# Second half's loads and squares moved into the first half's block loop, six conditioning columns moved into the mixer, last three squares summed apart

## The chip, the core and the metric

The kernel runs on one core of a Trainium2 chip. The metric is the device time of one execution in microseconds (us). A core has a matrix engine (PE, with its weight loads listed as PEld), a vector engine (DVE), a scalar engine (ACT), a general engine (POOL) and SyncE (SP), which issues most DMA transfers here; POOL issues some too.

## What is computed

The reference is a trunk of two layers over one sequence of 1024 positions and 1024 features, in float32. A conditioning vector c gives every layer six vectors of 1024 (shift, scale and gate for the token mixer and for the MLP).

```
cond = silu(c)
mod  = cond @ w_mod[i] + b_mod[i]            # six vectors: sh_m, sc_m, gt_m, sh_f, sc_f, gt_f
h = rms_norm(x, g) * (1 + sc_m) + sh_m
y = mixer(h)                                  # layer 0: recurrent, layer 1: pooling
x = x + gt_m * y
h = rms_norm(x, g) * (1 + sc_f) + sh_f
x = x + gt_f * (relu(h @ w1)**2 @ w2)
...
return rms_norm(x, final_norm_g)

# recurrent mixer of layer 0
gate = gelu(h @ w_y + b_y);  xr = conv4(h @ w_in + b_in)
r, i = sigmoid(blockdiag(xr, w_a)), sigmoid(blockdiag(xr, w_x))
a = exp(8 * r * log_sigmoid(lam));  u = sqrt(1 - a*a) * i * xr
y = (scan(a, u) * gate) @ w_out + b_out
```

## The kernel before

x lies transposed: 128 partitions hold a block of features, and there are 8 blocks (k or m = 0 to 7). The 1024 positions are two halves of 512 (h = 0, 1; tiles xa and xb). Every product is made of three matmuls of 128x128 weights with 512 positions: high part by high part, high by low, low by high (mm3, L188 to L190; the input norm's own in L401). Weights come as raw tiles of 512 KB (pool rawp, three buffers, shared with the conditioning columns), ACT casts the high part and DVE subtracts the low part (split_part, L180 and L181).

**Start.** The first loop of loads (L113 to L129) issues on SP, in the order of a string, the w_in pieces for features k (w_k) and for each block e the two raw conditioning tiles mw[e] of 2 x 512 KB (scale, then shift). SP works its queue in order. The *block loop* (L380 to L402) then runs over the 8 blocks of half 0: DVE makes scale and shift of a block from mw[k] (scale_of and bias_of, L335 to L339), ACT makes hh (high part of the normalised block), DVE hl (low part), and PE adds the block's 18 matmuls into the six accumulators ps6. The helper `after` (L321 to L328) ties each instruction of ACT, DVE and POOL in this stretch to the one before it on its engine, so the order there is that of the code, and all these lines show as L328. POOL issues accumulating DMAs (tile k of w_k) meanwhile. Behind the block loop stand the loads and splits of w_in 6 and 7, load_x(1) (four loads of 512 KB for xb, L409), the squares of xb (s1, L443 to L445: ACT squares, DVE adds them up), the evictions of ps6 to xr (conv_input, L426), the products of w_in 6 and 7 for half 0 (proj), rstd_bcast of s1 (L265 to L289; 4 matmuls with a column of ones, square root, reciprocal, and two matmuls with a diagonal dg that spread it), norm_split (L291) and the products of half 1.

**Mixer.** The loop at L556 runs over four heads hd, and over both halves in each: gates (L502 to L540) makes four sigmoid gates from w_g, then a chain through ACT, POOL, DVE to the scan; gelu_block (L542 to L546) multiplies two blocks of w_y products, taken through gelu on ACT. A stage is written (hd, h). Each split_unit loads one weight tile and then calls drip(n) with n = rate[0]: n *conditioning columns* for later (mod_steps, L216; mod_column, L205 to L207) each take a raw buffer, one load of 512 KB (mb) on SP, and one DVE pass over 128x1024. Columns come in the order gate of the mixer (0,2), then (0,4), (0,3), (0,5) for the MLP, then layer 1. rate[0] is hd. Three units load per head, so 0, 3, 6 and 9 columns are made. Outside the tied stretch a scheduler orders the instructions of each engine by the code's order, by buffers and by data.

**MLP of layer 0.** The wo loop (L586 to L599) adds the mixer's product to x and sums squares (ss); f1(0, 0) at L858 makes the first hidden chunk, with ffn_norm of half 1 (L571) inside it, on ss[1]; its four weight loads drip one column each (f1_jobs, L682), and drip_until(0, 5) at L859 makes those that are missing of the MLP's gate.

**End.** The last product of half 1, last 256 positions, goes through last_chunk (L1013): xb is updated on DVE, squared on ACT, summed on DVE for the letters V of the plan; the last square (X) has a tile of its own. rstd_row (L993 to L1002) multiplies both tiles by a 128x128 of ones, and ACT and DVE make root and reciprocal over 128x256; final_norm scales and stores.

## Time and profile before

| what | value |
|---|---|
| times of 3 runs | 1739.61, 1742.8, 1742.51 us (median 1742.51) |
| the profiled execution's own time | 1740.37 us |
| its span in the trace | 1738.5 us |
| mean granted TensorE clock | 0.994 of full speed |
| PE busy | 1690.5 us, 97% |
| DVE, ACT, POOL busy | 1358.9, 967.2, 492.3 us |
| HBM read, written | 181.79 MB, 4.19 MB |

The trace is that of one execution. A row of a timeline has start, duration, engine, line, operation, output<-inputs, shapes and, in square brackets, the idle time of the engine ahead of it with what ended it. The span covers the first to the last instruction; the execution's own time is 1.87 us longer. PE is busy for 97% of the span, so what is idle of PE is some 48 us, in stretches that can be listed one by one.

### The profile page before, as it was taken

The numbers are of one execution on the slowest core, as the hardware profiler recorded it, in microseconds if no ns is written. First come the engines' busy times: TensorE is split into PE (matmuls) and PEld (weight loads), VectorE is DVE, ScalarE is ACT, GpSimd is POOL, SyncE is SP. The second block draws the span as 40 slices with busy tenths as digits, with TensorE's granted clock in tenths as the row PEclk, the third lists the DMA queues.
The fourth block names the chain that finished last, engine by engine and source line by source line (L and its number), as shares of the span: only waits on it lengthen the run. The fifth ranks groups of instructions, "written<-read, shape, count | busy, mean of one in ns | idle before, by whom it ended". The sixth has DMA issues, their size and how long they took to land.

```text
span 1738.5 us, 20871 instructions
## 1 busy us (share of the span) xinstructions
PE 1690.5 (97%) x7472; PEld 1386.7 (80%) x7472; DVE 1358.9 (78%) x2115; ACT 967.2 (56%) x1660; POOL 492.3 (28%) x419
## 2 busy tenths in 40 slices
PE   6899999999999999999999999999999999999997
PEld 4687778877788888888888888888878787878787
DVE  7897867589898989897973898559696868687847
ACT  6588886555454454545457787745444454545432
POOL 2132343103241414151416333303140405041403
PEclk9999999999999999999999999999999999999999
DMA  9423425642423333332319888841111112120202
GB/s 337 168 93 104 143 85 162 143 119 83 136 72 123 95 99 109 96 117 89 123 37 198 202 192 179 190 118 61 49 59 39 61 38 70 39 69 29 80 6 97
DMA packets 63175, 187.33 MB, mean 108 GB/s; under 512 B 6752, under 2 KB 9184, under 8 KB 63072
## 3 DMA queue, kind: packets, MB, share of 16 engines
q1 hardware_dynamic: 47376, 157.43, 27.6%
q0 software_dynamic: 15696, 28.58, 9.9%
q8 instruction: 58, 0.95, 0.2%
q14 instruction: 45, 0.37, 0.1%
HBM read 181.79 MB, written 4.19 MB: 107 GB/s over the span
## 4 chain that ended last, share of the span: by engine, by line
PE 75%; DVE 10%; issue 3%; ACT 3%; DMA 2%; POOL 1%; DVEq 0%; ACTq 0%; POOLq 0%
PE mm L188 25%; PE mm L189 25%; PE mm L190 25%; DMA mb<-in_wmod 2%; DVE mb L207 1%; DVE xa L773 1%; DVE xb L773 1%; POOL xa L782 1%; DVE xcb L440 1%; DVE w_a_s L181 1%; ACT c L777 0%; DVE gate L530 0%; PE sm L272 0%; DVE w_y L181 0%; DVE w_s L181 0%
## 5 line engine op out<-in xcount | busy, mean ns | idle before, releaser
L188 PE MATMUL mm<-hh,w_w 128*128 128x512 f32 x1024 | 399.7, 390 | 0.9 <-DVE xa L773 0.9
L189 PE MATMUL mm<-hl,w_w 128*128 128x512 f32 x1024 | 399.3, 390 | 0.0
L190 PE MATMUL mm<-hh,w_w 128*128 128x512 f32 x1024 | 399.0, 390 | 0.0
L782 POOL TENSOR_TENSOR xb<-xb,c 128x512 f32<-128x512 f32 x104 | 150.0, 1442 | 625.4 <-ACT c L777 625.2
L188 PEld LDWEIGHTS mm<-hh,w_w 128*128 128x128 f32 x1024 | 192.6, 188 | 43.1 <-DVE xa L773 3.0
L190 PEld LDWEIGHTS mm<-hh,w_w 128*128 128x128 f32 x1024 | 192.6, 188 | 40.2
L189 PEld LDWEIGHTS mm<-hl,w_w 128*128 128x128 f32 x1024 | 192.5, 188 | 39.5
L782 POOL TENSOR_TENSOR xa<-xa,c 128x512 f32<-128x512 f32 x104 | 159.7, 1535 | 145.2 <-ACT c L777 145.2
L777 ACT ACTIVATE c<-c,mod 128x512 f32<-128x512 f32 x104 | 75.3, 724 | 202.6 <-DVE c L803 135.5
L623 ACT ACTIVATE relu<-mm 128x512 f32<-128x512 f32 x128 | 76.2, 596 | 144.7 <-PE mm L190 144.7
L207 DVE SCALAR_TENSOR_TENSOR mb<-mb,cond 128x1024 f32<-128x1024 f32 x80 | 114.5, 1434 | 47.9 <-DMA mb<-in_wmod 47.9
L773 DVE SCALAR_TENSOR_TENSOR xa<-mm,mod,xa 128x512 f32<-128x512 f32 x156 | 113.0, 742 | 25.8 <-POOL xa L782 25.8
L181 DVE TENSOR_TENSOR w_w<-raw_w,w_w 128x512 fp32r<-128x512 f32 x112 | 106.8, 962 | 12.4 <-ACT w_w L180 12.4
L165 POOL DMA_DIRECT2D w_w<-in_w x80 | 70.5, 900 | 151.0 <-ACT w_w L164 120.6
L613 DVE TENSOR_TENSOR u<-usq,u 128x512 fp32r<-128x512 f32 x102 | 70.2, 688 | 16.1 <-ACT u L612 15.8
L188 PE MATMUL mm<-u,w_a_a 128*128 128x512 f32 x200 | 79.1, 396 | 2.3 <-DVE xb L773 1.2
L188 PE MATMUL mm<-u,w_w 128*128 128x512 f32 (+1 forms) x224 | 80.9, 361 | 0.0
L189 PE MATMUL mm<-u,w_w 128*128 128x512 f32 (+1 forms) x224 | 80.5, 360 | 0.1
L190 PE MATMUL mm<-u,w_w 128*128 128x512 f32 (+1 forms) x224 | 80.4, 359 | 0.0
L180 ACT CAST w_w<-raw_w 128x512 fp32r<-128x512 f32 x112 | 65.1, 612 | 25.0 <-PE mm L190 17.3
L189 PE MATMUL mm<-u,w_a_a 128*128 128x512 f32 x200 | 78.0, 390 | 0.0
L190 PE MATMUL mm<-u,w_a_a 128*128 128x512 f32 x200 | 77.9, 389 | 0.0
(326 smaller groups left out, 4030.0 us busy)
## 6 DMA issues: line engine op xcount, KB each, us to landing
raw_w<-in_w SPq DMA_DIRECT2D x148, 512.0 KB, 3.5
mb<-in_wmod SPq DMA_DIRECT2D x80, 512.0 KB, 3.8
w_w<-in_w POOLq DMA_DIRECT2D x80, 256.0 KB, 5.5
mw<-in_wmod SPq DMA_DIRECT2D x16, 512.0 KB, 11.0
raw_in<-in_w_in SPq DMA_DIRECT2D x8, 512.0 KB, 7.0
raw_y<-in_w_y SPq DMA_DIRECT2D x8, 512.0 KB, 3.7
raw_o<-in_w_out SPq DMA_DIRECT2D x8, 512.0 KB, 4.2
outT<-o SPq DMA_DIRECT2D x12, 256.0 KB, 2.2
```

The source lines that it names most:

```text
L165: nc.gpsimd.dma_start(w[:, 1, 0:n], src, accum_op=ALU.add)
L180: S.copy(w[:, 0, 0:n], raw)
L181: (eng or V).tensor_sub(w[:, 1, 0:n], raw, w[:, 0, 0:n].bitcast(F32))
L188: PE.matmul(out=ps, lhsT=wh, rhs=rh, start=first, stop=False)
L189: PE.matmul(out=ps, lhsT=wh, rhs=rl, start=False, stop=False)
L190: PE.matmul(out=ps, lhsT=w[:, 1, c:c + P], rhs=rh, start=False, stop=last)
L207: V.scalar_tensor_tensor(raw, raw, 1.0, cond, op0=ALU.mult, op1=ALU.mult, accum_out=m[:, e:e + 1])
L613: eng.tensor_sub(u[n][:, 1, jj, :], src, u[n][:, 0, jj, :].bitcast(F32))
L623: S.activation(r, ps, AF.Relu)
L773: V.scalar_tensor_tensor(xb, ps, g[:, r + 4 * row:r + 4 * row + 1], xb, op0=ALU.mult, op1=ALU.add)
L777: S.activation(t, src, AF.Identity, scale=g[:, r + 4 * row:r + 4 * row + 1])
L782: G.tensor_add(xb, xb, t)
```

## The change

Four edits. The four loads of xb are issued between mw5 and mw6 instead of behind the block loop. The squares of xb and their sums are made by square1 inside the block loop, at k = 5 (blocks 0 to 2), k = 6 (3 to 5) and k = 7 (6 and 7), tied by `after` to the loop's order. The mixer's rate per unit becomes 0, 2, 3, 3 (6 columns more in all), and the four units of f1(0, 0) drip none. In the last chunk the plan has three squares of their own (X); the new class LastSumSq multiplies the running sum and each of the three by a column of ones as they come, into one accumulator, and rstd_bcast (128x2 and the dg matmuls) takes the place of rstd_row.

```diff
--- before.py
+++ after.py
@@ -110,7 +110,7 @@
         return part * n, part * n + n
 
     mw = [slot(f"mw{e}", (2, D)) for e in range(NB)]
-    for what in "0ww1w2w34567":
+    for what in "0ww1w2w345x67":
         if what == "w":
             q = len(k_raw)
             if q == 0:
@@ -122,6 +122,8 @@
                 for r, c0 in ((r1, 0), (r2, D)):
                     lo, hi = piece(r, q, part)
                     nc.sync.dma_start(r[:, lo:hi], w_k[q, :, c0 + lo:c0 + hi])
+        elif what == "x":
+            load_x(1)
         else:
             e = int(what)
             for j in (1, 0):
@@ -248,6 +250,7 @@
             self.name, self.n, self.plan, self.room = name, n, plan, room
             self.parts = {}
             self.i = 0
+            self.ps = None
 
         def add(self, xb):
             who = self.plan[self.i]
@@ -262,15 +265,36 @@
                 S.activation(sq, xb, AF.Square)
                 return (G if who == "G" else V).tensor_add(a, a, sq)
 
+    class LastSumSq(SumSq):
+
+
+        def add(self, xb):
+            if self.i == 0:
+                self.ps = small_ps()
+            if self.plan[self.i] == "V":
+                super().add(xb)
+                if "V" in self.plan[self.i:]:
+                    return
+                a = self.parts["V"]
+            else:
+                a = tmp("sq", self.n)
+                self.i += 1
+                S.activation(a, xb, AF.Square)
+            for q in range(self.n // P):
+                PE.matmul(out=self.ps[:, q:q + 1], lhsT=a[:, q * P:(q + 1) * P], rhs=ones[:, 0:1],
+                          start=(a is self.parts["V"] and q == 0), stop=(self.i == NB), skip_group_check=True)
+
     def rstd_bcast(ss, trace=None):
 
         nq = ss.n // P
         parts = list(ss.parts.values())
-        ps = small_ps()
-        for q in range(nq):
-            for pi, a in enumerate(parts):
-                PE.matmul(out=ps[:, q:q + 1], lhsT=a[:, q * P:(q + 1) * P], rhs=ones[:, 0:1],
-                          start=(pi == 0), stop=(pi == len(parts) - 1))
+        ps = ss.ps
+        if ps is None:
+            ps = small_ps()
+            for q in range(nq):
+                for pi, a in enumerate(parts):
+                    PE.matmul(out=ps[:, q:q + 1], lhsT=a[:, q * P:(q + 1) * P], rhs=ones[:, 0:1],
+                              start=(pi == 0), stop=(pi == len(parts) - 1))
         r = mp.tile([P, 4], F32, tag="rstd", name="rstd", bufs=2)
         root = S.activation(r[:, 0:nq], ps[:, 0:nq], AF.Sqrt, bias=eps, scale=1.0 / D)
         V.reciprocal(r[:, 0:nq], r[:, 0:nq])
@@ -370,6 +394,15 @@
     def normed(k):
         xn[k] = tmp("xn")
         after(V.tensor_mul, xn[k], x[0][:, k, :], bc0)
+
+    s1 = SumSq("m01")
+
+    def square1(k):
+        sq = tmp("sq")
+        after(S.activation, sq, x[1][:, k, :], AF.Square)
+        a = s1.parts.setdefault("V", sq)
+        if a is not sq:
+            after(V.tensor_add, a, a, sq)
 
     low = prepare(0)
     bias_of(0)
@@ -395,6 +428,8 @@
             prepare(k + 1)
         if k + 3 < NB:
             normed(k + 3)
+        for k1 in {5: (0, 1, 2), 6: (3, 4, 5), 7: (6, 7)}.get(k, ()):
+            square1(k1)
         for low, r in ((0, hh), (0, hl), (1, hh)):
             for u in range(6):
                 w, c = (w1_, u * P) if u < 4 else (w2_, odd * 256 + (u - 4) * P)
@@ -406,7 +441,6 @@
         behind.enter_context(tc.issue_after(tail_of[e].ins))
 
     uin = {m: split_unit(w_in[m], f"in{m}") for m in (6, 7)}
-    load_x(1)
     xc = [Blocks("xca"), Blocks("xcb")]
     edge = const.tile([P, NB, 3], F32, name="edge")
     xr3 = []
@@ -440,9 +474,6 @@
                 V.scalar_tensor_tensor(o, xr[:, k:k + H], vcol(f"cw{k}", m), o,
                                        op0=ALU.mult, op1=ALU.add)
 
-    s1 = SumSq("m01", plan="VVVVVVVV")
-    for k in range(NB):
-        s1.add(x[1][:, k, :])
     xr = [conv_input(m, ps6[m], 0) for m in range(6)]
     taken = last_traced(S)
     xr.append(conv_input(6, proj(uin[6], hh[0], hl[0]), 0))
@@ -554,7 +585,7 @@
             V.tensor_sub(yl[h][:, k, :], xc[h][:, k, :], yh[h][:, k, :].bitcast(F32))
 
     for hd in range(4):
-        rate[0] = hd
+        rate[0] = (0, 2, 3, 3)[hd]
         ug = split_unit(w_g[hd], f"g{hd}")
         uy = [split_unit(w_y[m], f"y{m}") for m in (2 * hd, 2 * hd + 1)]
         for h in range(2):
@@ -680,7 +711,7 @@
     DRIPS = (1, 1, 1, 1, 1, 1, 1, 1)
 
     def f1_jobs(i, c, eng=None):
-        return [partial(lambda j: split_unit(w1[i, c * 4 + j], f"w1_{i}_{c}_{j}", eng, DRIPS[j]), j) for j in range(4)]
+        return [partial(lambda j: split_unit(w1[i, c * 4 + j], f"w1_{i}_{c}_{j}", eng, 0 if (i, c) == (0, 0) else DRIPS[j]), j) for j in range(4)]
 
     def f2_jobs(i, c, eng=None):
         return [partial(lambda r: f2_weights(i, c, r, eng), r) for r in range(4)]
@@ -990,17 +1021,6 @@
     osrc = outT.rearrange("(b p) t -> p b t", p=P)
     units = [split_unit(w2[1, 7, dp], f"w2_1_7_{dp}") for dp in range(4)]
 
-    def rstd_row(ss):
-
-        parts = list(ss.parts.values())
-        ps = small_ps()[:, 0:ss.n]
-        for pi, a in enumerate(parts):
-            PE.matmul(out=ps, lhsT=ones, rhs=a, start=(pi == 0), stop=(pi == len(parts) - 1))
-        r = tmp("rrow", ss.n)
-        S.activation(r, ps, AF.Sqrt, bias=eps, scale=1.0 / D)
-        V.reciprocal(r, r)
-        return r
-
     def final_norm(bc, h, t0, n):
         per = H // n
         for k0 in range(0, NB, per):
@@ -1011,7 +1031,7 @@
             nc.sync.dma_start(osrc[:, k0:k0 + per, h * H + t0:h * H + t0 + n], o)
 
     def last_chunk(h, t0, n, plan, side=iter(())):
-        s = SumSq(f"o{h}{t0}", n, plan)
+        s = (LastSumSq if "X" in plan else SumSq)(f"o{h}{t0}", n, plan)
         for dp in range(4):
             f2_block(1, 7, units[dp], dp, h, s, t0, n)
             next(side, None)
@@ -1034,8 +1054,8 @@
     n1 = 256
     sa = last_chunk(0, 0, H, "VVVVVVVV")
     sb = last_chunk(1, 0, n1, "VVVVVVVV", once(lambda: final_norm(rstd_bcast(sa), 0, 0, H)))
-    sc = last_chunk(1, n1, H - n1, "VVVVVVVX", mid_norm())
-    final_norm(rstd_row(sc), 1, n1, H - n1)
+    sc = last_chunk(1, n1, H - n1, "VVVVVXXX", mid_norm())
+    final_norm(rstd_bcast(sc), 1, n1, H - n1)
 
 
 def _layout(inputs):
```

On DVE in the block loop, from the scale of block 6 on. mw is a raw conditioning tile, amix the scale, mod0_0 the shift, hl the low part of the half-0 block. Before:

```order
L328 ISA mw6_95,amix0_178<-mw6_95,cond_144,bmix1_180,vec_79 128x1024
L328 ISA amix0_178 128x1
L328 TENSOR_TENSOR hl0_1_185<-xn_317,hh0_1_183 128x512
L328 ISA mw6_95,mod0_0_179<-mw6_95,cond_144,vec_79 128x1024
L328 ISA mod0_0_179 128x1
L328 ISA mw7_96,amix0_178<-mw7_96,cond_144,bmix1_180,vec_79 128x1024
L328 ISA amix0_178 128x1
L328 TENSOR_TENSOR hl0_1_185<-xn_342,hh0_1_183 128x512
L328 ISA mw7_96,mod0_0_179<-mw7_96,cond_144,vec_79 128x1024
L328 ISA mod0_0_179 128x1
L328 TENSOR_TENSOR hl0_1_185<-xn_367,hh0_1_183 128x512
```

After (sq_396 is the sum of the squares of xb):

```order
L352 ISA mw6_95,amix0_182<-mw6_95,cond_148,bmix1_184,vec_79 128x1024
L352 ISA amix0_182 128x1
L352 TENSOR_TENSOR hl0_1_189<-xn_321,hh0_1_187 128x512
L352 TENSOR_TENSOR sq_396<-sq_396,sq_398 128x512
L352 TENSOR_TENSOR sq_396<-sq_396,sq_401 128x512
L352 ISA mw6_95,mod0_0_183<-mw6_95,cond_148,vec_79 128x1024
L352 ISA mod0_0_183 128x1
L352 ISA mw7_96,amix0_182<-mw7_96,cond_148,bmix1_184,vec_79 128x1024
L352 ISA amix0_182 128x1
L352 TENSOR_TENSOR hl0_1_189<-xn_346,hh0_1_187 128x512
L352 TENSOR_TENSOR sq_396<-sq_396,sq_427 128x512
L352 TENSOR_TENSOR sq_396<-sq_396,sq_430 128x512
```

Two adds of squares now stand between hl of block 5 and the shift of block 6, and the next adds behind hl of block 6; the scale of block 6 stands ahead of hl of block 5, as before.

On DVE in the mixer at stage (1,1), up to the second gate multiply. mb is a raw conditioning column, w_y4 and w_y5 are low parts of weights, gate is the chain to the scan. Before:

```order
L207 SCALAR_TENSOR_TENSOR mb0_4_0_1567,mod0_4_1566<-mb0_4_0_1567,cond_144 128x1024
L181 TENSOR_TENSOR w_y4_0_1554<-raw_y4_1546,w_y4_0_1554 128x512
L530 SCALAR_TENSOR_TENSOR gate_1427<-asq_1462,gate_1427 128x512
L181 TENSOR_TENSOR w_y4_512_1557<-raw_y4_1546,w_y4_512_1557 128x512
L530 SCALAR_TENSOR_TENSOR gate_1445<-asq_1465,gate_1445 128x512
L536 TENSOR_TENSOR gate_1436<-gate_1436,gate_1427 128x512
```

After:

```order
L209 SCALAR_TENSOR_TENSOR mb0_4_4_1579,mod0_4_1550<-mb0_4_4_1579,cond_148 128x1024
L183 TENSOR_TENSOR w_y4_0_1571<-raw_y4_1560,w_y4_0_1571 128x512
L209 SCALAR_TENSOR_TENSOR mb0_4_5_1582,mod0_4_1550<-mb0_4_5_1582,cond_148 128x1024
L561 SCALAR_TENSOR_TENSOR gate_1436<-asq_1471,gate_1436 128x512
L183 TENSOR_TENSOR w_y4_512_1574<-raw_y4_1560,w_y4_512_1574 128x512
L183 TENSOR_TENSOR w_y5_0_1588<-raw_y5_1577,w_y5_0_1588 128x512
L561 SCALAR_TENSOR_TENSOR gate_1454<-asq_1474,gate_1454 128x512
L567 TENSOR_TENSOR gate_1445<-gate_1445,gate_1436 128x512
```

One column more stands ahead of the first gate multiply, and the split of w_y5 ahead of the second.

On DVE at the end of the wo stage, up to the reciprocal of ffn_norm for half 1. ssq is the sum of squares, xb the updated half 1, raw_w2 a weight tile. Before:

```order
L263 TENSOR_TENSOR ssq_2167<-ssq_2167,sq_2748 128x512
L207 SCALAR_TENSOR_TENSOR mb0_5_6_2843,mod0_5_2400<-mb0_5_6_2843,cond_144 128x1024
L594 TENSOR_TENSOR xb_1_84<-xb_1_84,wo_2776 128x512
L207 SCALAR_TENSOR_TENSOR mb0_5_7_3190,mod0_5_2400<-mb0_5_7_3190,cond_144 128x1024
L263 TENSOR_TENSOR ssq_2167<-ssq_2167,sq_2779 128x512
L210 TENSOR_TENSOR mod0_5_2400<-mod0_5_2400,vec_79 128x8
L276 RECIPROCAL rstd_2896<-rstd_2896 128x4
```

After:

```order
L209 SCALAR_TENSOR_TENSOR mb1_1_0_2851,mod1_1_2850<-mb1_1_0_2851,cond_148 128x1024
L266 TENSOR_TENSOR ssq_2185<-ssq_2185,sq_2766 128x512
L755 TENSOR_TENSOR raw_w2_0_0_0_2847<-raw_w2_0_0_0_2847 128x256
L625 TENSOR_TENSOR xb_1_84<-xb_1_84,wo_2794 128x512
L266 TENSOR_TENSOR ssq_2185<-ssq_2185,sq_2797 128x512
L753 TENSOR_TENSOR raw_w2_0_0_1_3198<-raw_w2_0_0_1_3198 128x256
L755 TENSOR_TENSOR raw_w2_0_0_1_3198<-raw_w2_0_0_1_3198 128x256
L300 RECIPROCAL rstd_2904<-rstd_2904 128x4
```

Of the conditioning columns ahead of the last sum and of the reciprocal, three before, one is left (mb0_5_6, mb0_5_7 and the last addition to mod0_5 are gone from here).

## Rows read from the trace of the kernel before

**Rows 1.** The page's first section: busy us, share of the span, instructions.

```profile
PE 1690.5 (97%) x7472; PEld 1386.7 (80%) x7472; DVE 1358.9 (78%) x2115; ACT 967.2 (56%) x1660; POOL 492.3 (28%) x419
```

**Rows 2.** What PE waited for: us in total, times, longest us.

```profile
PE mm L188 <- ACT gelu L545: 6.1, 4, 1.9
```

**Rows 3.** Timeline of PE around the end of the block loop.

```profile
57.18 0.61 PE L401 MATMUL mm<-hh,k 128*128 128x512 f32 x2
61.83 0.80 PE L188 MATMUL mm<-hh,w_in 128*128 128x512 f32 x1 [4.04 <-ACT xr L426]
...
69.97 0.95 PE L272 MATMUL sm<-ones,ssqm01V 128*128 128x1 f32 x8
...
78.53 1.19 PE L188 MATMUL mm<-hh,w_in 128*128 128x512 f32 x4 [0.45 <-ACT hh L295]
```

**Rows 4.** Stretches: us, busy of PE, PEld, DVE, ACT, POOL, granted clock, DMA share.

```profile
60.48:67.31 6.83, 5.48 (x13) 4.37 (x14) 4.67 (x12) 6.83 (x13) 0.00 (x0) 0.50 0.04 17
...
364.27:367.68 3.41, 3.41 (x9) 2.65 (x10) 2.86 (x7) 0.26 (x1) 0.00 (x0) 0.50 0.28 112
```

**Rows 5.** DMA issues at 23.1 and at 27.3: KB, us to landing.

```profile
mw<-in_wmod SPq DMA_DIRECT2D x1, 512.0 KB, 16.2
...
mw<-in_wmod SPq DMA_DIRECT2D x1, 512.0 KB, 19.8
```

**Rows 6.** Timeline of ACT behind the block loop.

```profile
45.98 0.82 ACT L328 ACTIVATE hh<-xn,mod,amix 128x512 fp32r<-128x512 f32 x1 [1.96 <-DVE mod L328]
...
55.97 0.63 ACT L258 ACTIVATE ssqm01V<-xb 128x512 f32<-128x512 f32 x1 [1.42 <-DMA xb<-in_xT]
...
60.06 1.15 ACT L262 ACTIVATE sq<-xb 128x512 f32<-128x512 f32 x2 [0.27 <-DMA xb<-in_xT]
```

**Rows 7.** Timeline of DVE in the block loop.

```profile
44.05 0.69 DVE L328 TENSOR_TENSOR hl<-xn,hh 128x512 fp32r<-128x512 f32 x1 [0.47 <-ACT xn L328]
...
47.20 1.34 DVE L328 CUSTOM_DVE_ANT_0 mw<-mw,cond,bmix 128x1024 f32<-128x1024 f32 x1 [1.26 <-DMA mw<-in_wmod]
```

**Rows 8.** Timeline of DVE in the mixer, stages (1,0) and (1,1).

```profile
166.81 2.32 DVE L207 SCALAR_TENSOR_TENSOR mb<-mb,cond 128x1024 f32<-128x1024 f32 x1
...
181.30 1.21 DVE L207 SCALAR_TENSOR_TENSOR mb<-mb,cond 128x1024 f32<-128x1024 f32 x1
...
185.94 1.77 DVE L207 SCALAR_TENSOR_TENSOR mb<-mb,cond 128x1024 f32<-128x1024 f32 x1 [0.78 <-DMA mb<-in_wmod]
...
189.08 0.68 DVE L530 SCALAR_TENSOR_TENSOR gate<-asq,gate 128x512 f32<-128x512 f32 x1
```

**Rows 9.** Timeline of POOL at stage (1,0).

```profile
166.18 4.11 POOL L535 TENSOR_TENSOR gate<-gate,xca 128x512 f32<-128x512 f32 x2 [10.08 <-ACT gate L517]
```

**Rows 10.** Timeline of ACT at stage (1,1).

```profile
193.97 0.69 ACT L545 ACTIVATE gelu<-mm,vec 128x512 f32<-128x512 f32 x1
```

**Rows 11.** Timeline of PE at the w_y products of (1,1) and (2,1).

```profile
196.87 0.39 PE L188 MATMUL mm<-hh,w_y 128*128 128x512 f32 x1
...
233.31 0.50 PE L188 MATMUL mm<-hh,w_y 128*128 128x512 f32 x1 [1.87 <-ACT gelu L545]
```

**Rows 12.** DMA issues of the mixer's columns (page, section 6): KB, us to landing.

```profile
mb<-in_wmod SPq DMA_DIRECT2D x80, 512.0 KB, 3.8
```

**Rows 13.** Timeline of DVE at the last sums ahead of ffn_norm.

```profile
358.83 1.23 DVE L207 SCALAR_TENSOR_TENSOR mb<-mb,cond 128x1024 f32<-128x1024 f32 x1 [2.08 <-DMA mb<-in_wmod]
...
361.26 1.23 DVE L207 SCALAR_TENSOR_TENSOR mb<-mb,cond 128x1024 f32<-128x1024 f32 x1 [0.59 <-DMA mb<-in_wmod]
...
362.41 0.69 DVE L263 TENSOR_TENSOR ssq<-ssq,sq 128x512 f32<-128x512 f32 x1
```

**Rows 14.** Timeline of PE there.

```profile
363.24 1.02 PE L272 MATMUL sm<-ones,ssq 128*128 128x1 f32 x8 [3.94 <-DVE mod L210]
```

**Rows 15.** Timeline of all engines in the last chunk.

```profile
1728.45 0.70 PE L998 MATMUL sm<-ssqo1256X,ones 128*128 128x256 f32 x2 [0.20 <-ACT ssqo1256X L258]
...
1729.69 1.75 DVE L1001 RECIPROCAL rrow<-rrow 128x256 f32<-128x256 f32 x1 [1.80 <-ACT rrow L1000]
```

## The prediction

> **What bounds the kernel now.** The page's first section comes first: PE is busy for 97% of the span [rows 1], so only PE's idle stretches, some 48 us, and its slow stretches are to be had. The list of what PE waited for comes next; four waits for gelu in the mixer add up to 6.1 us [rows 2]. Then the timeline of PE shows where the others stand: 4.04 us behind the block loop, where the first product waits for an eviction on ACT [rows 3], and 3.94 us ahead of the statistics of half 1 in the MLP [rows 14]. Last the stretches with the granted clock: behind both waits it stands at 0.50, the lower of its two levels (1.2 GHz), for 6.83 and 3.41 us [rows 4]. In the first PE was busy for 5.48 us of it, in the second for all 3.41; at the full clock half of that would do, so 2.7 and 1.7 us go there. The edits touch these two places, the mixer, and the last few us.
>
> **The start: x ahead of mw6.** In the trace of before, the transfer issued at 23.1 lands 16.2 us later, at about 39.3, and the one issued at 27.3 lands 19.8 us later, at 47.2 [rows 5]. Between them lie the two of mw6: three transfers of 512 KB in 7.8 us, 2.6 each, while POOL's accumulating transfers run. When those are over, xb's four come faster: the first square starts at 55.97 and the one on the last piece at 60.06, three loads in 4.1, 1.4 each [rows 6]. SP's transfers land in the order of issue. After the change four of xb and then the scale half of mw6 follow mw5: 39.3 plus five transfers at 2.6 is 52.3, and 46.2 by 1.4 each. POOL's traffic is over only near 52, as the slow pace of before shows until in6 and in7, so I take 52.0. The next three, of mw6 and mw7, land at 53.3, 54.6 and 56.
>
> On DVE hl of block 5 (44.05 in before [rows 7]) stands behind the scale of block 6, as the order shows; before, that column had its data. Now it starts at 52.0 and takes 1.3 [rows 7], and hl follows at 53.3 to 54.0. PE, which has block 5's high part done by about 46.8, stands for some 7 us. From there DVE sets the pace: two adds at 0.69 each (the size of [rows 13]'s last row) to 55.4; shift of 6 to 56.4; hh on ACT, 0.82 [rows 6], to 57.2; scale of 7 to 57.7, hl of 6 to 58.4, three adds to 60.5, shift of 7 to 61.8, hh to 62.6, ACT's second pass and hl to 64.1. PE then has 12 matmuls left: two take 0.61 [rows 3] where one takes 0.39 [rows 11], so the pitch is 0.22 to 0.23, 2.7 in all, and the block loop ends near 67.3. It was 57.18 + 0.61 = 57.8 [rows 3]: 9.5 later.
>
> What follows gets shorter. The statistics of s1, 0.95 [rows 3], run at once; ACT, without casts and squares ahead of the evictions, frees the first accumulator meanwhile, so the 4.04 go. The product of w_in 6 takes 24 x 0.227 = 5.5 instead of 69.97 - 61.83 = 8.1 at the half clock: 67.3 + 0.95 + 5.5 = 73.7. From 69.97 to 78.53 lay 8.6 in before [rows 3]; without its 0.95, and without the wait of 0.45 for hh and a similar one for dg, whose work now lies under the product, 6.3 are left. Half 1 would start at 80.0, against 78.53: **+1.5**. Ends: a lower clock in the block loop after its long stalls is not excluded, since both long waits of before had one behind them, and costs up to 2.7 more; and if the dripping stalls overlap better, it is +0.5. Some of that vanishes in the first wait for gelu, 1.5 on average [rows 2], which ends on ACT and DVE; their half-1 normalisation starts about 0.9 later by the same chain. I take **+0.9** into the second half of the mixer.
>
> **The mixer: six columns more.** Heads 1 and 2 get 6 and 9 columns instead of 3 and 6. A column is one load, 3.8 from issue to landing in the middle [rows 12], and one DVE pass of 1.21 [rows 8]; the buffers are three, and a weight or column holds one until DVE and ACT are done. Work on DVE alone, 6 x 1.21 = 7.3, is hidden, since DVE is busy 78% of the span [rows 1]. What counts is a column that stands ahead of a gate multiply. At (1,1) the first gate multiply starts at 189.08 behind a column that waited 0.78 for its load [rows 8]; now a second column stands there, whose load can start only when the one ahead gives its buffer back, w_y4 and w_y5 holding the others. That is a load and a pass, 5.0 at most; 3.4 + 1.2 less the wait already there, about 4.4, is what I take. The gelu behind it starts at 193.97 and takes 0.69 [rows 10], so 194.7; PE starts the product that needs its accumulator at 196.87 [rows 11]: slack 2.2. So PE loses 2.2 here, which includes the 0.9 above, as a late PE only widens the slack. At (2,0) PE arrives later than before and what it waited for there, about 1.5, is met; the four waits together [rows 2] bound what can be given back. At (2,1) two columns stand ahead of the first gate multiply as before, but their loads queue behind one more. PE waited 1.87 there already [rows 11]. A lateness of **2.4** at the end of the mixer is my value; ends 0.5 (the loads come in time, and a gelu wait is saved) and 8 (nothing is hidden).
>
> **The MLP.** Of the columns ahead of the last sum of half 1, the two that waited 2.08 and 0.59 for their loads [rows 13] are gone; one is left, further ahead. DVE had been idle since 358.83 - 2.08 = 356.75 [rows 13]; from there an add, its square and the sum, 0.69 or less each, give 358.8 at the latest, instead of 363.1. Since earlier columns of that stretch are gone as well, it may be up to 2.6 sooner, 356.2. PE would have come to its statistics at 363.24 - 3.94 = 359.3 [rows 14] at the same place in its order, and somewhat sooner where the scheduler now puts them, 356.4 by my count. Between a wait of none and of 2.4 I take none, as the load that was waited for is what set this place: the 3.94 go, and the 1.7 of half clock behind them, **-5.6**; the other end, a wait of 2.4 that still brings the lower clock, is -1.5. The columns taken from f1(0, 0) cost nothing there; the three late ones move into layer 1's, which PE doesn't wait for.
>
> **The end.** The reciprocal over 128x256, 1.75 [rows 15], goes, and so do the two products with the 128x128 of ones, the last of which is 0.70 at 1728.45 [rows 15]. In come three sets of column products, a reciprocal, a cast and a subtraction over 128x2, two diagonals and two more products, each a few tenths with its hand-over. By what they replace (0.70 + 1.75) these chains are equal within 0.5: **0**, from -0.5 to +0.5.
>
> **The sum** against the profiled execution of 1740.37: +2.4 - 5.6 + 0 = -3.2, so 1737.2. That execution lies 2.14 below the median of the runs (1742.51), so against the median it is **1739.3**; with the ends of the terms (not all at once), 1736 to 1743.5.
>
> **Rivals.** *x costs nothing.* If mw6 lands near 46 (five loads at 1.4, the other end above), DVE isn't held, the block loop ends within 3 or so of 57.8 for the adds in it, and the 4.04 and 2.7 go: about 5.0 less than forecast, **1734.3**. Against it: the pace was 2.6 in that very stretch [rows 5].
>
> *The mixer's columns go one after another* (the slower side). Each load of the moved columns waits for a buffer that DVE frees late, and at (1,0), (1,1) and one stage of head 2 a load and a pass, 4.6, are paid in full, less 2.2 of slack once: 11.4 late instead of 2.4, **1748.3**. It decides from the point where the mixer's lateness passes 9.1 - there the sum is +3.5. For it: a pass took 2.32 at 166.81 [rows 8], beside POOL's gate multiplies of 166.18 to 170.29 [rows 9], where it took 1.21 at 181.30. The Trainium skill ("SBUF — State Buffer", section Who interferes with whom) says that a DVE instruction with two SBUF inputs contends with a GpSimd instruction that reads SBUF, and that PE and ACT never wait on either. By that rule the trace agrees, and it speaks against columns where POOL works: six at 1.1 more each would be 6.7 of DVE time. Against this rival: DVE has idle time ahead of the gates, and two of the four waits are there to swallow some.
>
> *The MLP's wait stays.* The one column left lands as late as the one at 358.83 did [rows 13], and PE stands for its sum as before: no -5.6, so **1744.9**. Against it: that column is the first of layer 1, issued ahead of a stretch with fewer loads.
>
> **How the numbers follow.** Chances: the forecast 0.45, x for nothing 0.20, the columns one after another 0.18, the MLP's wait 0.12, others 0.05. A measurement of this kernel can tell about 0.2%, 3.5 us, from no change. The forecast lies at -3.2, at this line: of its 0.45 I put 0.22 to faster. With x for nothing faster is 0.42; the rest of the forecast, the MLP's wait (+2.4) and a part of the others make 0.38 for the same; the columns' rival and what is left make 0.20 for slower. The range reaches from 1733.5, just past the faster rival, to 1747.0, past the MLP's rival and the first part of the slower one.
>
> **What would show it.** In the profile of the changed kernel: the scale of block 6 on DVE near 52 with a wait for its load, and PE standing some 7 us in the block loop; no wait for xr behind it and half 1 at 80; a second column with a load wait ahead of the gate multiply at (1,1), and PE waiting some 2 for gelu there; no wait of the statistics of half 1 near 356. Wrong would be: mw6 landing by 47, a PE wait above 5 in the mixer, or a wait of PE for the last sum in the MLP.

## The result, and the profile after

The changed kernel takes 1753.64 us (median of 4 runs, 1752.79 to 1754.21), the kernel before 1741.06 beside it: a ratio of 1.0072, 95% interval 1.0054 to 1.0089. It is 12.6 us slower, beyond the range's upper end. The profiled execution has a span of 1752.0 against 1738.5.

The page of after, first section (busy time, share of the span, instructions):

```profile
PE 1695.9 (97%) x7486; PEld 1391.3 (79%) x7486; DVE 1361.8 (78%) x2117; ACT 967.6 (55%) x1660; POOL 500.4 (29%) x419
```

Against [rows 1] PE is busy 5.4 us more, for nearly the same work, and idle 56.1 instead of 48.0. So two things need a cause: 8.1 us of waits, and 5.4 us in which PE was slow. The list of what PE waited for in after (total us, times, longest):

```profile
PE mm L190 <- ACT gelu L576: 10.5, 4, 6.0
PE mm L436 <- DVE hl L352: 7.8, 2, 7.6
...
PE sm L310 <- DVE dg L308: 5.3, 3, 2.4
...
PE mm L190 <- ACT hh L319: 2.6, 1, 2.6
```

The waits for an eviction behind the block loop [rows 3] and for the statistics of half 1 in the MLP [rows 14] are gone, as forecast. In their place stand 7.6 us inside the block loop (forecast), 2.6 behind it (not forecast), 10.5 for gelu where [rows 2] have 6.1, and 5.3 for dg in all the normalisations, where before has 2.5 (two waits).

The slow part shows in the windows of after (us, length, PE busy and matmuls, PEld, DVE, ACT, POOL, granted clock, DMA share, GB/s):

```profile
54.00:59.00 5.00, 4.57 (x11) 3.60 (x12) 4.43 (x8) 1.95 (x3) 0.00 (x0) 0.50 0.84 340
85.00:91.00 6.00, 5.74 (x14) 4.49 (x15) 6.00 (x11) 2.44 (x4) 0.00 (x0) 0.50 0.00 0
246.00:250.00 4.00, 4.00 (x10) 3.13 (x11) 4.00 (x7) 3.97 (x7) 0.00 (x0) 0.50 0.10 7
378.00:381.00 3.00, 3.00 (x9) 2.32 (x8) 3.00 (x6) 2.04 (x3) 0.00 (x0) 0.50 0.14 56
```

Ahead of the last chunk the clock stands at its lower level, 1.2 GHz, in four places, each behind a wait of PE. The kernel before has three such places: the two of [rows 4], and one behind its own wait at (2,1), which the prediction does not name. The windows of before, the first at the times of after's stall at 83, the second at (2,1), the third at the times of after's last one:

```profile
85.00:91.00 6.00, 6.00 (x29) 4.95 (x27) 5.87 (x11) 4.81 (x8) 0.00 (x0) 1.00 0.00 0
234.56:237.97 3.41, 3.41 (x9) 2.63 (x8) 3.41 (x7) 3.38 (x6) 0.00 (x0) 0.50 0.24 67
378.00:381.00 3.00, 3.00 (x14) 2.47 (x14) 2.97 (x6) 2.97 (x6) 0.00 (x0) 1.00 0.35 82
```

Fourteen matmuls instead of 29 in the 6 us from 85 are some 3 us of work not done. So the stretch at 60 was traded for one in the block loop and one at 85, the one in the MLP only moved, and the one at (2,1) got longer.

**Where the lateness arises.** By the same matmuls in both traces, after is 0.8 late at its first statistics already (12.74 against 11.96; in the other runs, whose first loads are the same, this lies between 11.87 and 12.59), 4.8 where half 1 starts, 8.3 behind the half clock that follows, 6.3 behind the first wait for gelu, 5.8 ahead of (1,1), 8.1 behind its stall, 13.1 to 13.5 behind the one at (2,1) and up to the MLP's last sum, 12.3 behind it and 12.6 at the end of layer 1; the span is 13.5 longer. One trace is good for some 2 us: that of the tail alone, whose code is before's up to the last chunk, is 2.7 early behind the mixer, 1.6 of it because its wait of 1.98 at (2,1) was not followed by the half clock and before's of 1.87 was.

### The profile page after: what moved, and what is told of

The parts are those of the page before. It is cut to its first block, busy times and chain, and to the rows that moved or that the text cites. A ratio compares the mean times of both kernels' runs of the same rounds, so it can differ in the third digit from the quotient of the medians.

```text
span 1752.0 us, 20898 instructions
## 1 busy us (share of the span) xinstructions
PE 1695.9 (97%) x7486; PEld 1391.3 (79%) x7486; DVE 1361.8 (78%) x2117; ACT 967.6 (55%) x1660; POOL 500.4 (29%) x419
## 4 chain that ended last, share of the span: by engine, by line
PE 80%; DVE 9%; DMA 4%; ACT 3%; issue 2%; POOL 1%; SPq 0%; DVEq 0%; ACTq 0%
PE mm L190 27%; PE mm L191 26%; PE mm L192 26%; DMA mw<-in_wmod 2%; DMA mb<-in_wmod 2%; DVE mb L209 1%; DVE xa L804 1%; DVE xb L804 1%; DMA raw_k<-in_w_k 1%; POOL xa L813 1%; DVE xca L474 1%; DVE w_a_s L183 1%; ACT c L808 0%; DVE w_s L183 0%; PE sm L296 0%
## 5 line engine op out<-in xcount | busy, mean ns | idle before, releaser
L192 PEld LDWEIGHTS mm<-hh,w_w 128*128 128x128 f32 x1024 | 192.5, 188 | 39.9
```

The costliest lines, as they stand in the source:

```text
L192: PE.matmul(out=ps, lhsT=w[:, 1, c:c + P], rhs=rh, start=False, stop=last)
```

## The experiments

Each expectation names its theories by letters. The ratio is always to the kernel before, run beside it on the same chip.

**The start alone.** The changed kernel with the old rate, the old drips and the old tail.

```diff
-        rate[0] = (0, 2, 3, 3)[hd]
+        rate[0] = hd
-                 eng, 0 if (i, c) == (0, 0) else DRIPS[j]), j)
+                 eng, DRIPS[j]), j)
-    sc = last_chunk(1, n1, H - n1, "VVVVVXXX", mid_norm())
+    sc = last_chunk(1, n1, H - n1, "VVVVVVVX", mid_norm())
```

> The start's part alone (xb ahead of mw6, squares in the block loop); rate, drips and the last chunk as before. Theory A (each part keeps its own cost): PE starts half 1 near 83, waits there for its normalisation and runs at the half clock behind it, is some 5 late behind the first gelu wait at (0,0), and the kernel ends +2 to +5 us. Rival B (a late PE only fills the gelu waits of the mixer): PE is as late at 95, but the lateness is under 1 us by the end of the mixer and the kernel ends within 1 us of before.

1746.32 against 1741.19, ratio 1.0032 (1.0020 to 1.0044): +5. PE of this kernel where half 1 starts:

```profile
83.31 1.20 PE L190 MATMUL mm<-hh,w_in 128*128 128x512 f32 x4 [2.75 <-ACT hh L319]
```

Behind the mixer the statistics of half 0 start at 337.93, against 332.99 in before: still 4.9 late. By its matmuls it is 4.8 late where half 1 starts, 6.8 ahead of the first wait for gelu, 5.3 behind it and 4.9 behind the second. So the first wait, 1.46 in before, is gone and swallowed 1.5, and the other three swallowed 0.4 together; the gelu waits add up to 4.4 us in three, against 6.1 in four.

**The columns alone.** The kernel before with the new rate and the new drips of f1(0, 0).

```diff
-        rate[0] = hd
+        rate[0] = (0, 2, 3, 3)[hd]
-                 eng, DRIPS[j]), j)
+                 eng, 0 if (i, c) == (0, 0) else DRIPS[j]), j)
```

> The columns' part alone: rates 0, 2, 3, 3 and no drips in f1(0, 0). Theory A (the columns' loads go one after another through the few raw buffers): gelu waits of about 2 at (1,1) and 4 to 6 at (2,1), lateness of PE behind the mixer +6 to +8; in the MLP the wait for the last sum goes, but the second late column stands inside the chain of the reciprocal and gives most of it back: -1 to -2; sum +4 to +7. Rival B (the stalls of the mixer came from the late start): gelu waits as before, under 2 each, and the kernel ends -1 to +1.

1747.21, ratio 1.0034 (1.0021 to 1.0047): +6. What PE waited for, and its longest gelu wait:

```profile
PE mm L188 <- ACT gelu L545: 13.3, 5, 5.6
...
PE sm L286 <- DVE dg L284: 5.9, 3, 3.0
```

```profile
241.66 0.79 PE L188 MATMUL mm<-hh,w_y 128*128 128x512 f32 x1 [5.59 <-ACT gelu L545]
```

By its matmuls it is 9.4 late behind the mixer and 9.0 behind the MLP's first statistics: the MLP edit gave 0.4. The execution that was traced took 1750.99, 3.8 more than the median, so its lateness is more than the typical one.

**The tail alone.** The kernel before with LastSumSq and the plan VVVVVXXX.

```diff
-    sc = last_chunk(1, n1, H - n1, "VVVVVVVX", mid_norm())
-    final_norm(rstd_row(sc), 1, n1, H - n1)
+    sc = last_chunk(1, n1, H - n1, "VVVVVXXX", mid_norm())
+    final_norm(rstd_bcast(sc), 1, n1, H - n1)
```

> The last chunk alone: three squares as sums of their own, column products, no row reciprocal. Theory A (the passes put into PE's stream delay the last product and what follows is equal): +1.0 to +1.4 us. Rival B (the prediction's term): 0, within 0.5.

1742.18, ratio 1.0003 (0.9994 to 1.0011): +1.0, which the times can't tell from none. The traces can. From one and the same product of the last chunk (at 1699.30 in before, 1698.34 here, 1711.94 in after) to the end it is 38.9 to 39.5 us in all eleven traces with the old tail and 39.9 to 40.2 in all four with the new one. So the new tail costs some 0.9. PE of this kernel:

```profile
1724.12 0.61 PE L282 MATMUL sm<-ones,ssqo1256V 128*128 128x1 f32 x4
1724.59 0.58 PE L282 MATMUL sm<-ones,sq 128*128 128x1 f32 x4
...
1726.67 0.61 PE L282 MATMUL sm<-ones,sq 128*128 128x1 f32 x4
...
1727.46 0.28 PE L190 MATMUL mm<-u,w_w 128*128 128x256 f32 x1
```

The last row is the last product. It starts 29.1 behind the product named above, against 27.3 in before, as three sets of column products now stand ahead of it; from there to the end it is 11.0 instead of 12.0. Start, columns and tail, +5.1, +6.0 and +1.0 by their medians, add to 12.1 of 12.6, so the three parts hardly work on each other.

**Fewer columns for head 1.** As the columns alone, but with its old rate for head 1.

```diff
-        rate[0] = hd
+        rate[0] = (0, 1, 3, 3)[hd]
```

> Columns alone with rates 0, 1, 3, 3: head 1 as before, head 2 with nine columns, three fewer moved in all. Theory A (what counts is the chain of loads of a stage): at (1,1) PE waits as before, none; at (2,1) 4 to 6; behind the mixer +3 to +5; in the MLP columns 5, 6 and 7 of the gate stand around the last sum and the reciprocal, so a wait of 2 to 4 stays there; sum +2 to +5. Rival B (it goes by the number of columns in the mixer): half the lateness of the full move, +3 behind the mixer, spread over both heads.

1740.87, ratio 0.9998 (0.9990 to 1.0006). PE waits for gelu 9.3 us in four, the longest 3.8 at (2,1); by its matmuls the mixer ends 5.6 late, and the MLP gives back 3.7. The traced execution, 1743.26, was 2.4 above the median. Against the columns alone it is 6.3 faster by the medians; by the traces 3.8 of that lie in the mixer (5.6 against 9.4) and the rest in the MLP. One wait grew at a head whose rate is the old one: 2.20 at (1,1), which no theory had. But the weights that load during head 1's stages are those of head 2 (w_y4 and w_y5 in the order shown at (1,1)), and their rate is the new one: a stage pays for the rate of the next head.

**The MLP's chain ahead of the columns.** The changed kernel; f2_weights of chunk 0, which drip, may issue only behind the DVE part of the reciprocal chain.

```diff
-        bc = rstd_bcast(ss)
+        bc = rstd_bcast(ss, norm_tr)
...
+        if (i, c) == (0, 0) and r > 0:
+            with tc.issue_after(norm_tr[V].ins):
+                return f2_weights_(i, c, r, eng)
```

> The changed kernel, with the DVE instructions of the chunk's second to fourth weight tiles and their columns queued behind the two diagonals of the half-1 statistics in the MLP; nothing else moves. Theory A (the second late column inside that chain holds DVE): PE's wait for dg near 376 goes, and the half clock behind it; 4 to 5.5 us faster than the changed kernel, that is +7 to +9 against before. Rival B (the wait goes to the next thing that is late there): a wait of 2 or more stays within 10 us of it, +11 to +13.

1749.11, ratio 1.0050 (1.0037 to 1.0063): 4.5 less than the changed kernel's 1753.64, and its trace is 5.1 earlier than after's from 390 on. Here

```profile
PE sm L310 <- DVE dg L308: 3.0, 2, 1.7
```

holds the long wait no more, while

```profile
PE mm L190 <- ACT gelu L576: 10.5, 4, 5.7
```

is as it was. By matmuls the lateness falls by 5.5 in the MLP here, from 12.7 to 7.2, where in after it falls by 1.2. This isolates why the MLP's part of the sum failed.

**The convolution behind the normalisation.** The changed kernel, with the taps of the first three blocks written behind norm_split.

```diff
-    for m in range(3):
-        conv(m, xr[m], 0)
...
-    for m in range(3, NB):
+    for m in range(NB):
```

> The changed kernel, with the first three convolutions of half 0 written behind the normalisation of half 1. Theory A (at the start PE waits for hh of half 1 because nine taps on DVE stand ahead of its normalisation): the wait of 2.6 near 83 and the half clock behind it go, half 1 starts near 80 to 81; 3 to 4.5 us faster than the changed kernel, +8 to +10 against before. Rival B (the convolutions are then late for the gates): the wait comes back as a gate or gelu wait by 150, and the kernel stays at +11 to +13.

1749.88, ratio 1.0057 (1.0045 to 1.0070). The wait at 83 is gone; the taps come later and hold up a weight's low part instead. DVE, then PE:

```profile
93.67 8.79 DVE L474 SCALAR_TENSOR_TENSOR xca<-xr,vec,xca 128x512 f32<-128x512 f32 x10
...
107.21 1.75 DVE L183 TENSOR_TENSOR w_in<-raw_in,w_in 128x512 fp32r<-128x512 f32 x1
```

```profile
109.02 0.80 PE L192 MATMUL mm<-hh,w_in 128*128 128x512 f32 x1 [6.45 <-DVE w_in L183]
```

The net gain against after is 3.8; it comes late, with a shorter gelu wait at (2,1), 2.52 instead of 6.00, as the mixer's stages ahead of that are no earlier than in after. The taps were what stood ahead of nt; moving them moved the wait.

**The MLP's columns away, nothing in the mixer.** The kernel before, f1(0, 0) and the first f2 weight tile without drips, the chain tied as above and the missing columns made behind it.

```diff
-                 eng, DRIPS[j]), j)
+                 eng, 0 if (i, c) == (0, 0) else DRIPS[j]), j)
...
-    drip_until(0, 5)
+    with tc.issue_after(norm_tr[V].ins):
+        drip_until(0, 5)
```

> The kernel before, with the same queueing, no drips in f1(0, 0) nor in the chunk's first weight tile, and the columns still missing of the MLP's gate behind the diagonals. Theory A (the MLP's wait is an order of DVE alone, and no column has to move into the mixer for it): the wait of 3.9 near 363 and the half clock behind it go, -4.5 to -5.6 against before. Rival B (the gate's columns come too late for the chunk's result): a wait on the update of x near 400 to 430 takes its place, -2 to +2.

1740.24, ratio 0.9998 (0.9989 to 1.0007). The wait of [rows 14] is gone and the trace is 8.0 early at 392, but 4.9 at 498 and only 1.5 from 600 on. New waits take them, on the update of x:

```profile
PE mm L188 <- DVE xa L780: 10.8, 10, 1.8
```

where before has 6.8 in seven. The columns then run among layer 0's next chunks and delay DVE there. A gain at 363 is real only if the columns go where nothing is late.

**The evictions ahead of the squares.** The kernel of the last run, with the evictions of ps6 written ahead of xb's squares.

```diff
+    xr = [conv_input(m, ps6[m], 0) for m in range(6)]
+    taken = last_traced(S)
     s1 = SumSq("m01", plan="VVVVVVVV")
     for k in range(NB):
         s1.add(x[1][:, k, :])
-    xr = [conv_input(m, ps6[m], 0) for m in range(6)]
-    taken = last_traced(S)
```

> The same, and at the start the six evictions of the accumulators written ahead of the squares of xb; the loads keep their order. Theory A (the 4.0 us behind the block loop are the eight squares on ACT ahead of the evictions): that wait shrinks to under 1 and the half clock behind it goes; half 1 starts 3 to 5 earlier, and 3 to 5 less than the run without it, -8 to -10 against before. Rival B (the statistics of xb come later by as much): PE waits for the squares or for hh of half 1 instead; 0 to -1 against the run without it.

1738.78, ratio 0.9988 (0.9980 to 0.9997). The wait of 4.04 [rows 3] shrinks to 0.63, and half 1 waits instead:

```profile
77.93 2.07 PE L188 MATMUL mm<-hh,w_in 128*128 128x512 f32 x4 [5.67 <-ACT hh L295]
```

**Passes without loads.** The kernel before, with six columns' worth of DVE work in heads 1 and 2 on data that is there, and no load.

```diff
         drip(rate[0] if drips is None else drips)
+        if drips is None and rate[0] in (1, 2) and name[0] in "gy":
+            for c in (0, H):
+                V.scalar_tensor_tensor(tmp("fake"), cond[:, c:c + H], 1.0,
+                                       cond[:, c:c + H], ..., accum_out=fake)
```

> The kernel before, with one more DVE pass per weight tile in the mixer's heads 1 and 2 (six in all, each as two halves of 512 over a tile that is already there, written to a scratch tile), and no load nor raw buffer with it; these passes feed nothing, and all real columns stay as before. Theory A (the mixer's stalls come from loads that wait for a raw buffer): gelu waits as before, lateness behind the mixer under 2, kernel within 0 to +2 of before. Rival B (they come from DVE time ahead of the gates): stalls at (1,1) and (2,1) as in the columns-alone run, +5 to +8 behind the mixer.

1754.39, ratio 1.0072 (1.0059 to 1.0085), which neither theory gave. Nothing holds these passes back, so they stand together ahead of a stage's chain, and PE waits 4.44 at (1,0) and 7.16 at (2,0), not at (1,1) and (2,1) as in after. It shows that DVE time in the wrong place costs as well, and does not tell loads from passes.

**Loads without passes.** The same place, with the load and the buffer, and a copy of 128x8 in place of the pass.

```diff
+            extra = rawp.tile([P, D + 256], F32, tag="raw", name="extra")[:, 0:D]
+            nc.sync.dma_start(extra, wmod[1, 5, rate[0]])
+            V.tensor_copy(tiny, extra[:, 0:8])
```

> The kernel before, with one more raw buffer and load of 512 KB per weight tile in the mixer's heads 1 and 2 (six in all), and a DVE copy of 128x8 in place of the pass of 128x1024; what they load feeds nothing, and all real columns stay as before. Theory A (a moved column costs by its load, which waits for a buffer and holds up the column behind it): waits for gelu at (1,1) or (2,1) grow to 3 or more, 4 to 8 late behind the mixer, +4 to +8 against before. Rival B (it costs by DVE's pass of 1.2 ahead of a gate multiply): gelu waits as before, under 2 late, 0 to +2.

1746.70 against 1740.44, ratio 1.0033 (1.0020 to 1.0045): +6.3, against +6.0 for the columns alone. PE:

```profile
180.72 0.51 PE L193 MATMUL mm<-hh,w_y 128*128 128x512 f32 x1 [3.13 <-ACT gelu L550]
...
220.44 0.80 PE L193 MATMUL mm<-hh,w_y 128*128 128x512 f32 x1 [5.19 <-ACT gelu L550]
```

So the loads and the buffers suffice for a cost of this size. The stages are (1,0) and (2,0), so the path is not the same one in detail. Which of the two, load or buffer, weighs more stays open: a fourth raw buffer, for which there was no room in the kernel as it is, was not tried.

**The columns beside w_out.** The kernel before with the chain tied, f1(0, 0) without drips, and more columns in the wo loop.

```diff
-                if m0 == 0:
+                if m0 == 0 or h == 0 or m < 6:
                     drip(1)
```

> The kernel before, with the six columns of the MLP's gate made in the second half of the output projection (one more per product of m = 4 to 7 of half 0, and of m = 4 and 5 of half 1) instead of in the mixer or in f1(0, 0), and the queueing behind the diagonals. Theory A (the columns need a stage where DVE waits for PE anyway and where raw buffers are free; before, DVE stands idle for most of 295 to 335): mixer as before, no wait near 363 nor half clock, no new waits in the first chunk; -4 to -6 against before. Rival B (loads share the queue with w_out's accumulating transfers and hold up w1's first tiles): a wait of PE for weights near 330 to 345 of 3 or more, -1 to +3.

1739.99, ratio 0.9995 (0.9986 to 1.0004). The wait for the MLP's sum falls to 0.29, but a column's load, beside w_out's accumulating transfers, is late for half 0's sum. DVE, then PE:

```profile
323.32 1.23 DVE L207 SCALAR_TENSOR_TENSOR mb<-mb,cond 128x1024 f32<-128x1024 f32 x1 [3.92 <-DMA mb<-in_wmod]
```

```profile
335.35 1.02 PE L272 MATMUL sm<-ones,ssq 128*128 128x1 f32 x8 [1.54 <-DVE ssq L263]
...
360.89 1.02 PE L272 MATMUL sm<-ones,ssq 128*128 128x1 f32 x8 [0.29 <-DVE ssq L263]
```

Behind the first, the granted clock averages 0.72 from 336 to 342, and most of the gain goes there.

**x behind mw7.** The start alone, but x's loads issue behind mw7 and all squares come at k = 7.

```diff
-    for what in "0ww1w2w345x67":
+    for what in "0ww1w2w34567x":
-        for k1 in {5: (0, 1, 2), 6: (3, 4, 5), 7: (6, 7)}.get(k, ()):
+        for k1 in {7: range(8)}.get(k, ()):
```

> The start's part alone, with the four loads of xb behind mw7 instead of ahead of mw6 and all eight squares at the last block. Theory A (the start's cost is that mw6 lands ten later and hl of block 5 stands behind it on DVE): no wait of 7.6 in the block loop, which ends near 58 as before; the statistics then wait for the squares, and half 1 starts 0 to 3 earlier than before; kernel -3 to +1. Rival B (the cost is the squares in the tied order, wherever the loads stand): half 1 starts at 81 or later, +3 to +6.

1738.25 against 1741.13, ratio 0.9986 (0.9977 to 0.9995). There is no wait of 7.6, and what is left behind the block loop is short:

```profile
59.03 1.02 PE L296 MATMUL sm<-ones,sq 128*128 128x1 f32 x8 [1.28 <-DVE sq L352]
60.63 0.50 PE L190 MATMUL mm<-hh,w_in 128*128 128x512 f32 x1 [0.57 <-ACT xr L460]
...
74.43 1.21 PE L190 MATMUL mm<-hh,w_in 128*128 128x512 f32 x4 [0.55 <-ACT hh L319]
```

Half 1 starts 4.1 earlier than [rows 3], 8.9 earlier than in after. So the order of the loads, with the squares put behind them, turned the start's edit from +5 to -3. How much the new place of the squares did by itself was not taken apart; the wait that went is the one that ended on mw6's load.

**Both repairs.** x behind mw7, the old rate in the mixer, the old tail, three columns more in the wo loop (m = 4 to 6 of half 0), the chain tied, f1(0, 0) and the first f2 weight tile without drips.

```diff
-                if m0 == 0:
+                if m0 == 0 or h == 0 and m < 7:
                     drip(1)
...
+    with tc.issue_after(norm_tr[V].ins):
+        drip_until(0, 5)
```

> The start with xb behind mw7 and all squares at the last block, together with three of the six columns in the second half of the output projection and three behind the diagonals in the first chunk. Theory A (the two gains lie in different stages and add, and three late columns are few enough for either place): no wait near 360 and none of 1 or more near 330; -5 to -8 against before. Rival B (what the MLP's wait gives is lost again to the columns, wherever they go): -2 to -3.5, as the start's part alone.

1730.22 (1729.6 to 1731.56, 5 runs) against 1740.44, ratio 0.9942 (0.9929 to 0.9955): 10.2 faster, better than both kernels, and more than either theory gave. By its matmuls it is 5.7 early behind the mixer, 1.6 of it because no half clock follows its wait at (2,1), and 9.5 at 1000. A window of it, with that of before behind it:

```profile
280.00:400.00 120.00, 119.80 (x536) 98.96 (x535) 86.75 (x148) 73.00 (x123) 15.72 (x18) 1.00 0.56 146
```

```profile
280.00:400.00 120.00, 116.06 (x513) 95.89 (x512) 80.68 (x138) 67.90 (x114) 13.96 (x16) 0.99 0.53 141
```

PE does 23 matmuls more in these 120 us and is idle for 0.2. The waits near 330 and 360 are both gone. That the columns cost nothing here, with x behind mw7, and did beside w_out in the run above, is measured as a pair of kernels; which of the differences (how many columns, beside which half, PE 5 us earlier) does it was not taken apart.

## Why the prediction was wrong, step by step

**The start: the right stall, the wrong next step.** DVE in the block loop of after:

```profile
52.42 1.34 DVE L352 CUSTOM_DVE_ANT_0 mw<-mw,cond,bmix 128x1024 f32<-128x1024 f32 x1 [9.35 <-DMA mw<-in_wmod]
53.69 0.69 DVE L352 TENSOR_TENSOR hl<-xn,hh 128x512 fp32r<-128x512 f32 x1
...
72.97 3.11 DVE L474 SCALAR_TENSOR_TENSOR xca<-xr,vec,xca 128x512 f32<-128x512 f32 x3
76.08 5.82 DVE L474 SCALAR_TENSOR_TENSOR xca<-xr,vec,xca 128x512 f32<-128x512 f32 x4
81.83 0.73 DVE L318 SCALAR_TENSOR_TENSOR nt<-xb,amix,sm 128x512 f32<-128x512 f32 x1
```

The scale of block 6 came at 52.42 (forecast 52.0), PE stood 7.59 (some 7), and the statistics of s1, which run at its end, started at 68.27 (67.3). The step that failed is "half 1 would start at 80.0": I counted PE's own work and took the first normalised block as ready. PE:

```profile
80.36 0.39 PE L192 MATMUL mm<-hh,w_in 128*128 128x512 f32 x1
83.37 1.27 PE L190 MATMUL mm<-hh,w_in 128*128 128x512 f32 x4 [2.62 <-ACT hh L319]
85.26 0.79 PE L191 MATMUL mm<-hl,w_in 128*128 128x512 f32 x1 [0.62 <-DVE hl L320]
```

DVE is at seven convolution taps from 72.97 on, ahead of nt at 81.83. They read xr, so they follow the evictions, and those start at 67.52 on ACT, behind the block loop, where before they started at 61.11. Taps stood ahead of nt in before too, with nt at 76.98. So with evictions 6.4 late nt is 4.9 late and half 1 4.8 late; PE's 24 matmuls at the full clock were done at 80.7, close to the forecast, and were no longer what ends last. The taps are also slow: of the seven, three took 0.74 and four 1.76 to 1.78, all four while POOL split w_in. DVE, then POOL:

```profile
78.44 1.78 DVE L474 SCALAR_TENSOR_TENSOR xca<-xr,vec,xca 128x512 f32<-128x512 f32 x1
...
76.13 5.22 POOL L183 TENSOR_TENSOR w_in<-raw_in,w_in 128x512 fp32r<-128x512 f32 x3 [0.59 <-ACT w_in L182]
```

At 0.74 each nt would come near 77.7, and half 1's first product, 1.55 behind nt in before, near 79.3, ahead of PE: an estimate, as no run moved POOL's splits. And both waits, at 54 and at 83, brought the lower clock; the ends named it for the block loop alone. The +1.5 became +4.8, and 8.3 behind the second stretch. That "some of that vanishes in the first wait for gelu" was right, 1.5 in the start alone; what is more than that stays, as the waits behind it end on chains of ACT and DVE that are late too.

**The mixer: the mechanism right, the size 13.5 instead of 2.4.** The 2.4 was the lateness behind the mixer, start included, and after is 13.5 late there. Of this 5.8 are there ahead of (1,1), where 0.9 was forecast, and 7.7 come at (1,1) and (2,1), where 1.5 was. The stall at (1,1), 2.04, is the one forecast (2.2), and the column ahead of its gate is the second:

```profile
192.78 1.23 DVE L209 SCALAR_TENSOR_TENSOR mb<-mb,cond 128x1024 f32<-128x1024 f32 x1 [1.14 <-DMA mb<-in_wmod]
...
197.68 1.23 DVE L209 SCALAR_TENSOR_TENSOR mb<-mb,cond 128x1024 f32<-128x1024 f32 x1 [2.23 <-DMA mb<-in_wmod]
198.83 0.69 DVE L561 SCALAR_TENSOR_TENSOR gate<-asq,gate 128x512 f32<-128x512 f32 x1
...
232.39 2.06 DVE L209 SCALAR_TENSOR_TENSOR mb<-mb,cond 128x1024 f32<-128x1024 f32 x1
...
238.94 1.23 DVE L209 SCALAR_TENSOR_TENSOR mb<-mb,cond 128x1024 f32<-128x1024 f32 x1 [3.88 <-DMA mb<-in_wmod]
```

The term that failed is (2,1), which I priced at nothing because two columns stood there before. Its last two rows are the slower rival's mechanism, to the letter: the first column's pass ends at 234.4 and gives its buffer back, the load of the second is issued at 234.48 and lands 4.4 us later, and the gate multiply stands behind it until 240.09. PE:

```profile
204.89 0.50 PE L190 MATMUL mm<-hh,w_y 128*128 128x512 f32 x1 [2.04 <-ACT gelu L576]
...
245.72 0.79 PE L190 MATMUL mm<-hh,w_y 128*128 128x512 f32 x1 [6.00 <-ACT gelu L576]
```

6.00 instead of 1.87 [rows 11], and a half clock behind it that is longer than before's and for which the mixer had no term. A wait above 5 in the mixer was named as a sign of being wrong. Both kernels make three columns per weight here, as the weights that load in this stage are head 3's; what changed is when the buffers come free. This rival should have had more than 0.18: a load queued "behind one more" in a pool of three is a load that waits for the pass ahead of it. The loads without passes give the same +6 with hardly any DVE work, so the DVE time that I hid behind 78% was not the point; the passes without loads warn that it is not free either.

**The MLP: the sum came in time, the chain behind it did not.** PE reaches its statistics without a wait at 370.08, as forecast. The step that failed is "the 3.94 go, and the 1.7 of half clock behind them". DVE of after, from the last sum on:

```profile
369.25 0.69 DVE L266 TENSOR_TENSOR ssq<-ssq,sq 128x512 f32<-128x512 f32 x1 [0.70 <-ACT sq L265]
...
371.65 0.17 DVE L303 CAST rstdh<-rstd 128x4 fp32r<-128x4 f32 x1
374.41 1.23 DVE L209 SCALAR_TENSOR_TENSOR mb<-mb,cond 128x1024 f32<-128x1024 f32 x1 [2.59 <-DMA mb<-in_wmod]
375.56 0.16 DVE L304 TENSOR_TENSOR rstd<-rstd,rstdh 128x4 f32<-128x4 f32 x1
375.64 0.68 DVE L308 TENSOR_TENSOR dg<-ident,rstdh 128x512 fp32r<-128x512 f32 x1
```

A second late column stands between the cast and the subtraction of the reciprocal, two instructions of 0.17. For 2.6 us DVE waits for its load, with dg behind it; PE waits 2.40 for dg at 376.38, and the clock falls to 0.50. I had counted the columns ahead of the sum and not those behind it; the built order showed this one. The lateness falls by 1.2 instead of 5.6. With the chain tied it falls by 5.5, and the kernel is 4.5 faster than after, which settles the cause.

**The tail: +0.9 instead of 0.** The step that failed is "these chains are equal within 0.5". The chain behind the last product did get shorter, by 0.9. But three sets of column products stand in PE's order ahead of that product, at 0.58 to 0.61 each and not "a few tenths", and put it off by 1.8.

**Slips in the sums.** At (1,1), 3.4 + 1.2 less 0.78 is 3.8 and not 4.4, so the loss by that chain was 1.6, and that the measured 2.04 lies close to 2.2 is in part luck. In the block loop, 64.1 + 2.7 is 66.8 and not 67.3, while the shift of block 6 got 1.0 where that of block 7 got 1.3. In the slower rival, three times 4.6 less 2.2 is 11.6 and not 11.4. None of these decides anything.

**In sum:** 5.8 late ahead of (1,1) instead of 0.9, another 7.7 in the mixer instead of 1.5, MLP -1.2 instead of -5.6, tail +0.9 instead of 0. Most waits that an edit took away came back elsewhere, and each of after's four longest waits from the block loop on (7.59, 2.62, 6.00 and 2.40) was followed by the lower clock.

## What to carry to other kernels

When an edit makes one input early, ask which input it pushes back: SP's 313 transfers landed in the order of issue, before and after, so a load for later belongs behind the last one that is needed first. A prefetch into a small shared pool can cost the next load's wait for a buffer, even where its work is hidden; and read every row between the pieces of a short chain, not only those ahead of it. A wait that ends on a chain as late as you are absorbs little: of 6.8 us, four waits took 1.9. And what stands in PE's order ahead of the last product costs its whole time.

## What the runs showed of the hardware

- Some waits of PE of 1.5 to 2.6 us were followed by the lower clock: 1.54 at 335.35 of the columns beside w_out by 0.72 from 336 to 342; in after 2.62 and 0.62 at 83 to 85 by 0.50 from 85 to 91, and 2.40 at 376.38 by 0.50 from 378 to 381. There the price of such a wait about doubled. In the run with x behind mw7 the waits of 1.28 and 0.57 near 60 were followed by 0.57 from 62 to 66. It isn't certain for any one wait: behind the 2.04 at 204.89 and the 1.58 at 223.09 of after the clock stayed at 1.00, and at (2,1) before's 1.87 was followed by 0.50 and the 1.98 of the tail alone was not, in the same code.
- The same column pass took 1.23 at 220.30 of after, with POOL idle, and 2.06 at 232.39, beside POOL's multiply of 231.47 to 233.36. The Trainium skill ("SBUF — State Buffer", section Who interferes with whom) says that a DVE instruction with two SBUF inputs contends with a GpSimd instruction that reads SBUF; the trace agrees, though the two rows could differ in other ways as well. The taps above, 0.74 and 1.78, agree too. Where DVE came first, at 192.78, its pass took 1.23 and POOL's multiply from 193.12 on was the long one, 1.79 against 1.04 at 214.57.
